# Output projections of a two-layer encoder trunk: two plain blocks and seven pairs, sums of the rows on GpSimd

## The chip, the cores and the metric

One core of one Trainium2 chip runs the whole program. The metric is the device time of one execution in microseconds: the median of the runs, 2163.85 for the kernel before (three runs, 2161.11 to 2164.45). The profile is of one further execution, with a time of its own.

## The reference

Two batches (256 and 512 rows, 768 together) go through an even and an odd layer of width 2048 with the same weights, in float32. Each layer ends with one output projection, whose result is added to the layer's input:

```
z = _rmsnorm(x, g) @ w_in
... the branches: attention and Fourier mixing (even), short convolution and spatial gate (odd),
... each multiplied by its SiLU gate
return x + jnp.concatenate([a, fo], axis=-1) @ w_out       # even
return x + jnp.concatenate([co, so], axis=-1) @ w_out      # odd
```

The concatenated, gated rows are what the change is about: 2048 features by 768 rows, which a 2048 x 2048 matrix multiplies.

## The kernel before

Everything stands transposed: a row block k of 128 features is a tile of 128 partitions by 768 rows, in two halves of 384 (s = 0, 1). There are 16 row blocks and 16 output blocks b. For precision each operand is split into a high and a low part: `split` (L130 to L132) copies on ScalarE (L131, hi) and subtracts on VectorE (L132, lo), and `three` (L117) issues three matmuls for every product. Weights come by DMA into `wr`, are split into `wh` and `wl` of 512 columns, and `Weights.ahead` does so four tiles before TensorE uses one (`RING`).

Blocks are made in two ways. *Plain*: `Stream.duo` takes two output blocks at once, 16 row blocks by 2 halves by 2 outputs by 3 matmuls, 192 in all, with 8 weight tiles. *In pairs*: `strassen` makes a pair of output blocks from seven products of half the size (Winograd's form): 7 x 8 x 3 = 168 matmuls with 14 weight tiles, of which four products first sum weights on VectorE (L196 to L202). Its left operands are the quarters of the rows, A11, A12, A21, A22 (feature half by row half), and three sums, S1 = A21 + A22, S2 = S1 - A11, S3 = A11 - A21; the seventh product needs S4 = A12 - S2, which here stands in the place of A21. The order of the products is A11, S1, S2, A12, S3, A22, S4. The sums must be formed and split before the first pair.

`Out.run` makes an output projection: two duos (blocks 0 to 3), then six pairs. Before the duos `load_cat` fills the slots of all 32 half row blocks from the stored gated rows (`cat`) and splits them; row blocks still on chip (`kept`) are split from there. Beside the first duo `build_sums` loads the rows a second time, into the slots of the sums; VectorE forms the four sums (L394 to L397) and splits three; the fourth, S4, is stored to memory (`s4d`, L398). Before the second duo everything pending is issued (`pipe.flush`). During the second duo, `done` loads S4 back into the place of A21 and splits it. In the even projection the slots of the sums (numbers 64 to 111) lie in the pool `late`, which takes over the memory of the attention's pool, tile by tile as those come free. In the odd projection `move` gives each quarter and sum the slots of operands of the pair before, in the order in which that pair frees them (`FREED`).

What sets the order: TensorE's is that of the program. The other engines and the DMA queue (all DMAs go out on SP) are put in order by a planner that goes by the order of the program and by what is ready in its own estimate. Generators spawned on `pipe` are stepped when the TensorE time counted in the program has come, so a helper's place in the program is between certain matmuls. In the even projection the result also gets squared on ScalarE (L786, L789) and added up on GpSimd (L790), for the norm of the odd layer.

Of the kernel before, what the change touches and what calls it, by code (L numbers as in the profile page):

```python
# [10 lines left out]
F32 = mybir.dt.float32  # L11
# [15 lines left out]
HT = H // P  # L27
BUILD = (4, 5, 6, 7, 0, 1, 2, 3)
BUILD_AT = 5.0
WIDTH = (TP, TS)  # L30
RING = 4
LOOK = 4
PLAIN = (0, 1, 2, 3)
PAIRS_E = ((8, 9), (10, 11), (12, 13), (14, 15), (4, 5), (6, 7))
PAIRS_O = ((4, 5), (6, 7), (8, 9), (10, 11), (12, 13), (14, 15))
PW = T + 4
# [56 lines left out]
def trunk(ctx, tc, x_t, w_in_e, w_fn, w_out_e, w_in_o, w_sv, w_out_o, w_f, w_st, b_s, sink, rel_bias,  # L93
# [62 lines left out]
    class Weights:  # L156
# [65 lines left out]
    def out_order(src, layer, pairs):  # L222
        plain = [(src, layer, b, q) for i in range(0, len(PLAIN), 2) for q in range(4) for b in PLAIN[i:i + 2]]
        return plain + [(src, layer, b, q) for b in pairs for q in range(14)]
# [30 lines left out]
    def x_slots(k, s):  # L255
        xs[k][s] = slots(quarter(k, s))
# [104 lines left out]
    kept = {}  # L361

    def load_cat(order):
        for k, s in order:
            x_slots(k, s)
            if k in kept:
                split(*xs[k][s], kept[k][:, SL[s]])
            else:
                fill(k, s, cat[k][:, SL[s]])
        kept.clear()  # L370
# [3 lines left out]
    def ev():  # L374
        return late[0].tile([P, H], F32, name="ev", bufs=4)
# [30 lines left out]
    def fill(k, h, src, g=None):  # L406
        at = where[quarter(k, h)]
        t = slot(at[1], F32)
        nc.sync.dma_start(out=t, in_=src)
        at[1], spare[0] = spare[0], at[1]  # L410
        x_slots(k, h)
        if g is None:
            split(*xs[k][h], t)
        else:
            split_gain(k, h, t, g)

    class Out:

        def __init__(self, n, pairs, first, last, res, result):
            self.n, self.pairs, self.res, self.result = n, pairs, res, result
            self.tags = (first, last, first)

        def run(self):
            st = Stream(self.n)

            def load(k, h, t):
                nc.sync.dma_start(out=t, in_=cat[k][:, SL[h]])

            def done(k, s):
                if s == 1 and k < KH:
                    fill(k, 1, s4d[k])

            pipe.spawn(build_sums(load, sums, BUILD, BUILD_AT))
            for i, tags in zip(range(0, len(PLAIN), 2), self.tags):
                duo = PLAIN[i:i + 2]
                last = i + 2 == len(PLAIN)
                if last:
                    pipe.flush()  # L440
                st.duo(duo, tags, done if last else None)
                for b in duo:
                    for h, z in enumerate(st.take(b)):
                        res = ev()
                        nc.sync.dma_start(out=res, in_=self.res[b][:, SL[h]])
                        nc.vector.tensor_add(out=res, in0=z, in1=res)
                        self.result(b, h, res)
            lent[0] = True
            for b in self.pairs:
                self.r = [big(i)[:, :T] for i in range(2)]  # L450
                for r, c in zip(self.r, b):
                    nc.sync.dma_start(out=r, in_=self.res[c])
                strassen(self.n, b, sums, ev, self, self.tags[-1])
            lent[0] = False
# [18 lines left out]
    def strassen(n, b, sums, ev, sink, tags):  # L473


        left = (
            [xs[j][0] for j in range(KH)], sums[1], sums[2], [xs[j + KH][0] for j in range(KH)],
            sums[3], [xs[j + KH][1] for j in range(KH)], [xs[j][1] for j in range(KH)],
        )
        acc = {}  # L480
        for i, at in enumerate((0, 2, 1, 0, 1, 3, 2)):
# [3 lines left out]
            for half in range(2):  # L485
                w = weights.at[n, b, 2 * i + half]
                weights.ahead(w + RING)
                for k in range(4):
                    j = 4 * half + k
                    three(acc[at], cols(weights.tiles[w], k), left[i][j], first and j == 0, j == KH - 1, not first)  # L490
                    pipe.tick()
# [172 lines left out]
    with tc.tile_pool(name="attn", bufs=1) as pool:  # L664
# [115 lines left out]

        load_cat([(k, s) for k in range(KT) for s in range(2)])

# [12 lines left out]
    sums = {i: [None] * KH for i in (1, 2, 3)}  # L795
    Out(1, PAIRS_E, (4, 5, 6, 7), (0, 1, 2, 3), x_t, keep_sum).run()

# [35 lines left out]
    if True:  # L833
# [124 lines left out]
    sums = {i: [None] * KH for i in (1, 2, 3)}  # L958
    Out(3, PAIRS_O, (0, 1, 2, 3), (4, 5, 6, 7), x1, finish).run()

# [79 lines left out]
```

## Time and profile before

| | |
|---|---|
| median of 3 runs | 2163.85 us |
| profiled execution | 2162.2 us, its span 2160.4 us |
| TensorE busy | 2120.9 us, 98% of the span, 12034 matmuls |
| VectorE busy | 1429.5 us, 66% |
| ScalarE busy | 898.9 us, 42% |
| GpSimd busy | 75.0 us, 3%, 75 instructions |
| granted TensorE clock | 0.995 on the mean |

The span runs from the first to the last instruction in the profile; the execution's time is 1.8 us longer. TensorE's share is an average: what matters for this change are two stretches, the even output projection (from about 790 to 1053 us) and the odd one (from about 1890 to the end). In the rows, `PE` is TensorE, `DVE` VectorE, `ACT` ScalarE, `POOL` GpSimd, `SPq` the DMA queue.

### The profile page before, as it was taken

To read this page: it belongs to the slowest core of one execution; us is meant where nothing else is said; L and a number is where in the kernel's file an instruction comes from. 1 tells how busy PE (TensorE), PEld (TensorE's weight loads), DVE (VectorE), ACT (ScalarE), POOL (GpSimd) and SP (SyncE) were. 2 spreads that over 40 slices of the span, in tenths; PEclk is the share of its full clock that TensorE was granted. 3 is DMA by queue.
4 is the path that set the end of the run, shared out by engine and by line. 5 is a ranking of instruction groups with operands and counts; after the bars stand their busy time and mean duration, and the time that the engine had idled before them with its cause. 6 is when DMAs were issued, how large, how long until landed. Compare 5 with 4: busy or idle time off the path is not lost.

```text
span 2160.4 us, 31653 instructions
## 1 busy us (share of the span) xinstructions
PE 2120.9 (98%) x12034; PEld 2074.6 (96%) x12034; DVE 1429.5 (66%) x2466; ACT 898.9 (42%) x1761; POOL 75.0 (3%) x75
## 2 busy tenths in 40 slices
PE   7999999999999998999899999999999999999999
PEld 5899999999999998999888999999999999999999
DVE  8535755745746768666795666666666777796665
ACT  6323443443444464333544433333334554553332
POOL 5000000000000000122100000000000000000000
PEclk9999999999999999999999999999999999999999
DMA  6522112122122148344946322222222332494342
GB/s 220 145 71 77 59 65 76 50 75 66 59 66 76 49 158 275 109 137 137 312 169 194 114 72 86 86 86 76 76 76 86 105 105 97 132 305 153 119 135 74
DMA packets 116512, 250.03 MB, mean 116 GB/s; under 512 B 12636, under 2 KB 72200, under 8 KB 116360
## 3 DMA queue, kind: packets, MB, share of 16 engines
q1 hardware_dynamic: 116360, 248.01, 35.3%
q8 instruction: 94, 1.54, 0.3%
q14 instruction: 58, 0.48, 0.1%
HBM read 210.19 MB, written 40.91 MB: 116 GB/s over the span
## 4 chain that ended last, share of the span: by engine, by line
PE 90%; DVE 3%; DMA 3%; ACT 2%; issue 1%; SPq 0%; DVEq 0%; ACTq 0%
PE bank L117 89%; DMA slot<-cat 1%; PE bank L127 1%; DMA xr<-in_x_t_dram 1%; DMA s<-slot 1%; DVE slot L268 1%; DVE slot L132 1%; DVE wl L132 0%; ACT sc L730 0%; DVE slot L395 0%; DVE slot L397 0%; ACT L730 0%; ACT L350 0%; DVE slot L396 0%; DVE slot L394 0%
## 5 line engine op out<-in xcount | busy, mean ns | idle before, releaser
L117 PE MATMUL bank<-slot,wh 128*128 128x384 f32 x6848 | 1747.0, 336 | 1.3 <-DVE ev L504 1.2
L117 PEld LDWEIGHTS bank<-slot,wh 128*128 128x128 f32 x6848 | 1236.1, 188 | 2.1 <-issue 1.5
L117 PE MATMUL bank<-slot,wl 128*128 128x384 f32 x3424 | 1150.0, 336 | 8.3 <-DVE wl L132 8.3
L131 ACT CAST wh<-wr 128x512 fp32r<-128x512 f32 x728 | 447.9, 620 | 875.8 <-PE bank L117 698.7
L132 DVE TENSOR_TENSOR wl<-wr,wh 128x512 fp32r<-128x512 f32 x728 | 504.8, 697 | 364.2 <-ACT wh L131 351.5
L117 PEld LDWEIGHTS bank<-slot,wl 128*128 128x128 f32 x3424 | 643.4, 188 | 9.6 <-DVE wl L132 9.6
L117 PE MATMUL bank<-wh,slot 128*128 128x512 f32 x576 | 187.1, 403 | 11.3 <-DVE slot L268 5.9
L117 PEld LDWEIGHTS bank<-wh,slot 128*128 128x128 f32 x576 | 111.0, 193 | 37.8 <-DVE slot L268 7.6
L131 ACT CAST slot<-slot 128x384 fp32r<-128x384 f32 x176 | 87.2, 512 | 108.0 <-DVE slot L132 37.4
L132 DVE TENSOR_TENSOR slot<-slot,slot 128x384 fp32r<-128x384 f32 x176 | 97.3, 557 | 31.9 <-ACT slot L131 24.3
L117 PE MATMUL bank<-wl,slot 128*128 128x512 f32 x288 | 115.3, 401 | 1.1 <-DVE wl L132 1.1
L689 DVE RECIPROCAL nrt<-nrt 128x384 f32<-128x384 f32 x32 | 81.6, 2549 | 4.8 <-ACT nrt L688 4.8
L117 PEld LDWEIGHTS bank<-wl,slot 128*128 128x128 f32 x288 | 55.7, 193 | 13.7 <-DVE wl L132 1.6
L345 DVE TENSOR_TENSOR row<-bank,rr 128x384 f32<-128x384 f32 x40 | 22.3, 557 | 39.6 <-PE bank L117 39.6
L200 DVE TENSOR_TENSOR wr<-wr 128x1024 f32<-128x1024 f32 x36 | 47.6, 1322 | 1.2
L202 DVE TENSOR_TENSOR wr<-wr 128x1024 f32<-128x1024 f32 x36 | 44.1, 1226 | 1.2
L196 DVE TENSOR_TENSOR wr<-wr 128x1024 f32<-128x1024 f32 x36 | 44.0, 1221 | 0.5
L198 DVE TENSOR_TENSOR wr<-wr 128x1024 f32<-128x1024 f32 x36 | 43.9, 1220 | 0.4
L790 POOL TENSOR_TENSOR rr<-rr,slot 128x384 f32<-128x384 f32 x24 | 35.3, 1473 | 130.2 <-ACT slot L789 130.2
L502 DVE TENSOR_TENSOR ev<-bank,ev 128x384 f32<-128x384 f32 x36 | 20.1, 558 | 28.7 <-PE bank L117 28.7
L507 DVE TENSOR_TENSOR ev<-ev,bank 128x384 f32<-128x384 f32 x36 | 19.9, 554 | 28.6 <-PE bank L117 28.6
L268 DVE SCALAR_TENSOR_TENSOR slot<-xr,sm,slot 128x384 fp32r<-128x384 f32 x32 | 36.5, 1184 | 3.2 <-ACT slot L267 3.2
(170 smaller groups left out, 1391.6 us busy)
## 6 DMA issues: line engine op xcount, KB each, us to landing
wr<-in_w_in_o_dram SPq DMA_DIRECT2D x96, 512.0 KB, 3.7
wr<-in_w_in_e_dram SPq DMA_DIRECT2D x72, 512.0 KB, 3.7
slot<-cat SPq DMA_DIRECT2D x120, 192.0 KB, 4.2
wr<-in_w_out_e_dram SPq DMA_DIRECT2D x32, 512.0 KB, 3.9
wr<-in_w_out_o_dram SPq DMA_DIRECT2D x32, 512.0 KB, 3.9
slot<-x SPq DMA_DIRECT2D x64, 192.0 KB, 4.2
wr<-in_w_sv_dram SPq DMA_DIRECT2D x16, 512.0 KB, 4.6
xr<-in_x_t_dram SPq DMA_DIRECT2D x15, 384.0 KB, 5.5
```

Of the source, the lines that this page charges most:

```text
L117: nc.tensor.matmul(out, lhsT=lhs, rhs=rhs, start=start, stop=stop, skip_group_check=go_on)
L127: nc.tensor.transpose(out=out, in_=in_, identity=ident)
L131: nc.scalar.copy(out=hi, in_=src)
L132: nc.vector.tensor_sub(out=lo, in0=src, in1=hi.bitcast(F32))
L196: nc.vector.tensor_sub(out=w11, in0=w12, in1=w11)
L198: nc.vector.tensor_sub(out=w11, in0=w22, in1=w11)
L200: nc.vector.tensor_sub(out=w12, in0=w22, in1=w12)
L202: nc.vector.tensor_sub(out=w21, in0=w11, in1=w21)
L268: nc.vector.scalar_tensor_tensor(out=lo, in0=src, scalar=g, in1=hi.bitcast(F32), op0=ALU.mult, op1=ALU.subtract)
L345: nc.vector.tensor_mul(out=out[:, SL[s]], in0=z[s], in1=rr[:, SL[s]])
L689: nc.vector.reciprocal(out=rt, in_=rt)
L790: nc.gpsimd.tensor_add(out=rr[:, SL[h]], in0=rr[:, SL[h]], in1=sq)
```

## The change

Both projections make one duo (blocks 0 and 1) and seven pairs. The rows are loaded once: `load_cat` loads each half row block as it is (`raws`) into the first four of the six slots of its sums, and splits from there into the slots of the quarters; rows still on chip are split by `split_kept`. `form`, begun 10 us (even) or 4 us (odd) after the duo starts, makes S1 on VectorE and S2, S3 and S4 on GpSimd, and splits S1. `place`, begun after the duo's eighth row block, splits S2, S4 and S3 of one row block after the other. S4 is not stored any more. In the odd projection the slots freed first now go to the sums.

```diff
-PLAIN = (0, 1, 2, 3)
-PAIRS_E = ((8, 9), (10, 11), (12, 13), (14, 15), (4, 5), (6, 7))
-PAIRS_O = ((4, 5), (6, 7), (8, 9), (10, 11), (12, 13), (14, 15))
+BUILD_E, BUILD_O = (4, 5, 6, 7, 0, 1, 2, 3), range(8)
+PLAIN = (0, 1)
+PAIRS_E = ((8, 9), (10, 11), (12, 13), (14, 15), (2, 3), (4, 5), (6, 7))
+PAIRS_O = ((2, 3), (4, 5), (6, 7), (8, 9), (10, 11), (12, 13), (14, 15))
...
+    def split_kept():
+        for k in sorted(kept):
+            for s in range(2):
+                x_slots(k, s)
+                split(*xs[k][s], kept[k][:, SL[s]])
     def load_cat(order):
         for k, s in order:
-            x_slots(k, s)
-            if k in kept:
-                split(*xs[k][s], kept[k][:, SL[s]])
-            else:
-                fill(k, s, cat[k][:, SL[s]])
+            j = k % KH
+            i = ((0, 1) if k < KH else (3, 2))[s]
+            t = raws[j, i] = slot([o for r in ("S1", "S2", "S3") for o in where[r, j]][i], F32)
+            nc.sync.dma_start(out=t, in_=cat[k][:, SL[s]])
+            if k not in kept:
+                x_slots(k, s)
+                split(*xs[k][s], t)
...
+        def form(self):
+            self.t = {}
+            for j in self.build:
+                ids = self.ids[j]
+                a0, a1, b1, b0 = (raws[j, i] for i in range(4))
+                nc.vector.tensor_add(out=b1, in0=a1, in1=b1)
+                t = self.t[j] = slot(ids[4], F32)
+                nc.gpsimd.tensor_sub(out=t, in0=b1, in1=a0)
+                nc.gpsimd.tensor_sub(out=a1, in0=a0, in1=a1)
+                nc.gpsimd.tensor_sub(out=b0, in0=b0, in1=t)
+                self.put(1, j, b1, ids[5])
+                spare[0] = ids[2]
+                yield 1.0
+        def place(self):
+            for j in self.build:
+                ids = self.ids[j]
+                self.put(2, j, self.t[j], ids[0])
+                spare[0] = ids[4]
+                x_slots(j, 1)
+                split(*xs[j][1], raws[j, 3])
+                self.put(3, j, raws[j, 1], ids[3])
+                spare[0] = ids[1]
+                yield 2.6
         def run(self):
             st = Stream(self.n)
             def done(k, s):
-                if s == 1 and k < KH:
-                    fill(k, 1, s4d[k])
-            pipe.spawn(build_sums(load, sums, BUILD, BUILD_AT))
+                if s == 1 and k == KH - 1:
+                    pipe.spawn(self.place(), 0.5)
+            pipe.spawn(self.form(), self.begin)
+            st.duo(PLAIN, self.first, done)
...
-        load_cat([(k, s) for k in range(KT) for s in range(2)])
+        split_kept()
...
+    load_cat([(k, s) for k in range(KT) for s in range(2)])
+    Out(1, PAIRS_E, BUILD_E, 10.0, (4, 5, 6, 7), (0, 1, 2, 3), x_t, keep_sum).run()
...
-        move("A11", "A21", "A12", "A22", "S1", "S2", "S3")
+        move("S1", "S2", "S3", "A11", "A21", "A12", "A22")
+        split_kept()
...
+    Out(3, PAIRS_O, BUILD_O, 4.0, (0, 1, 2, 3), (4, 5, 6, 7), x1, finish).run()
```

## Rows read from the trace of the kernel before

**Rows 1.** The page, part 4: shares of the chain that ended last, by engine.
```profile
PE 90%; DVE 3%; DMA 3%; ACT 2%; issue 1%; SPq 0%; DVEq 0%; ACTq 0%
```

**Rows 2.** Timeline of GpSimd in the even pairs: start, us, engine, line, operation [idle before].
```profile
895.86 1.01 POOL L790 TENSOR_TENSOR rr<-rr,slot 128x384 f32<-128x384 f32 x1 [5.01 <-ACT slot L789]
...
925.01 1.02 POOL L790 TENSOR_TENSOR rr<-rr,slot 128x384 f32<-128x384 f32 x1 [13.88 <-ACT slot L789]
```

**Rows 3.** Timeline of TensorE, even projection and just after it.
```profile
847.77 0.44 PE L117 MATMUL bank<-slot,wl 128*128 128x384 f32 x1 [3.06 <-DVE wl L132]
851.18 0.69 PE L117 MATMUL bank<-slot,wl 128*128 128x384 f32 x1 [2.62 <-DVE wl L132]
...
1057.12 1.22 PE L117 MATMUL bank<-wh,slot 128*128 128x512 f32 x2 [3.79 <-DVE slot L268]
```

**Rows 4.** Timeline of VectorE ahead of the even projection.
```profile
786.16 0.56 DVE L345 TENSOR_TENSOR row<-bank,rr 128x384 f32<-128x384 f32 x1 [1.52 <-PE bank L117]
...
806.55 0.95 DVE L354 TENSOR_TENSOR at<-row,at 128x768 f32<-128x768 f32 x1
```

**Rows 5.** Windows: length, busy us of PE, PEld, DVE, ACT, POOL (instructions), PEclk, DMA, GB/s.
```profile
2100.00:2129.16 29.16, 29.16 (x170) 29.16 (x169) 18.73 (x28) 9.09 (x15) 0.00 (x0) 1.00 0.33 109
850.00:855.00 5.00, 3.82 (x12) 3.82 (x13) 4.65 (x9) 3.21 (x7) 1.99 (x1) 0.50 0.88 285
787.00:851.00 64.00, 58.51 (x336) 57.87 (x335) 54.83 (x107) 37.17 (x76) 3.04 (x2) 0.98 0.88 291
1894.00:1957.30 63.30, 59.50 (x340) 58.50 (x338) 59.84 (x123) 30.16 (x62) 0.00 (x0) 1.00 0.85 281
```

**Rows 6.** Timeline of TensorE, odd projection: its waits.
```profile
1907.31 0.59 PE L117 MATMUL bank<-slot,wh 128*128 128x384 f32 x2 [1.18 <-DVE ev L504]
...
1921.86 0.44 PE L117 MATMUL bank<-slot,wl 128*128 128x384 f32 x1 [0.93 <-DVE wl L132]
...
1957.27 0.44 PE L117 MATMUL bank<-slot,wl 128*128 128x384 f32 x1 [1.69 <-DVE wl L132]
```

**Rows 7.** The page, part 6: DMA issues, count, KB each, us to landing.
```profile
slot<-cat SPq DMA_DIRECT2D x120, 192.0 KB, 4.2
...
slot<-s SPq DMA_DIRECT2D x24, 192.0 KB, 3.6
```

**Rows 8.** Timeline of ScalarE: the last product of attention.
```profile
777.84 0.48 ACT L752 COPY at<-bank 128x384 f32<-128x384 f32 x1 [0.62 <-PE bank L117]
```

**Rows 9.** Timeline of VectorE in the odd projection's first duo.
```profile
1926.88 0.69 DVE L132 TENSOR_TENSOR wl<-wr,wh 128x512 fp32r<-128x512 f32 x1
1927.49 0.55 DVE L132 TENSOR_TENSOR slot<-slot,slot 128x384 fp32r<-128x384 f32 x1
1927.96 0.68 DVE L132 TENSOR_TENSOR wl<-wr,wh 128x512 fp32r<-128x512 f32 x1
```

**Rows 10.** Timelines of VectorE and GpSimd in an even pair.
```profile
904.15 1.22 DVE L196 TENSOR_TENSOR wr<-wr 128x1024 f32<-128x1024 f32 x1
905.40 1.92 DVE L200 TENSOR_TENSOR wr<-wr 128x1024 f32<-128x1024 f32 x1
...
904.19 2.05 POOL L790 TENSOR_TENSOR rr<-rr,slot 128x384 f32<-128x384 f32 x1 [1.21 <-ACT slot L789]
```

**Rows 11.** Timeline of all engines in the even projection's second duo.
```profile
849.28 2.70 POOL L790 TENSOR_TENSOR rr<-rr,ev 128x384 f32<-128x384 f32 x1 [4.28 <-ACT ev L789]
849.50 0.55 DVE L397 TENSOR_TENSOR slot<-slot,slot 128x384 f32<-128x384 f32 x1
...
851.24 1.16 DVE L132 TENSOR_TENSOR slot<-slot,slot 128x384 fp32r<-128x384 f32 x1
```

**Rows 12.** Timeline of all engines at the kernel's start.
```profile
15.33 8.75 POOL L536 TENSOR_TENSOR acc<-acc,sq 128x768 f32<-128x768 f32 x4 [0.41 <-ACT sq L534]
...
18.04 6.98 DVE L268 SCALAR_TENSOR_TENSOR slot<-xr,sm,slot 128x384 fp32r<-128x384 f32 x4
...
25.54 1.14 DVE L268 SCALAR_TENSOR_TENSOR slot<-xr,sm,slot 128x384 fp32r<-128x384 f32 x2
```

More of the change, by code (lines that the diff above doesn't have):

```diff
@@ L27 @@
 HT = H // P
-BUILD = (4, 5, 6, 7, 0, 1, 2, 3)
-BUILD_AT = 5.0
+BUILD_E, BUILD_O = (4, 5, 6, 7, 0, 1, 2, 3), range(8)
 WIDTH = (TP, TS)
@@ L222, in out_order @@
     def out_order(src, layer, pairs):
-        plain = [(src, layer, b, q) for i in range(0, len(PLAIN), 2) for q in range(4) for b in PLAIN[i:i + 2]]
+        plain = [(src, layer, b, q) for q in range(4) for b in PLAIN]
         return plain + [(src, layer, b, q) for b in pairs for q in range(14)]
@@ L361, in trunk @@
     kept = {}
+    raws = {}
+    def split_kept():
[3 more added lines that the diff above has]
+                split(*xs[k][s], kept[k][:, SL[s]])
     def load_cat(order):
         for k, s in order:
-            x_slots(k, s)
-            if k in kept:
-                split(*xs[k][s], kept[k][:, SL[s]])
-            else:
-                fill(k, s, cat[k][:, SL[s]])
+            j = k % KH
[5 more added lines that the diff above has]
+                split(*xs[k][s], t)
         kept.clear()
@@ L417, in trunk, with __init__ @@
     class Out:
-        def __init__(self, n, pairs, first, last, res, result):
-            self.n, self.pairs, self.res, self.result = n, pairs, res, result
-            self.tags = (first, last, first)
+        def __init__(self, n, pairs, build, begin, first, last, res, result):
+            self.n, self.pairs, self.build, self.res, self.result = n, pairs, build, res, result
+            self.begin, self.first, self.last = begin, first, last
+            self.ids = {j: [i for r in ("S1", "S2", "S3") for i in where[r, j]] for j in build}
@@ new lines, in put @@
+        def put(self, i, j, src, hi):
+            where[f"S{i}", j] = [hi, spare[0]]
+            sums[i][j] = slots((f"S{i}", j))
+            split(*sums[i][j], src)
+        def form(self):
[11 more added lines that the diff above has]
+                yield 1.0
@@ L425, in run @@
+        def place(self):
[8 more added lines that the diff above has]
+                yield 2.6
         def run(self):
             st = Stream(self.n)
-            def load(k, h, t):
-                nc.sync.dma_start(out=t, in_=cat[k][:, SL[h]])
@@ L431, in done @@
             def done(k, s):
-                if s == 1 and k < KH:
-                    fill(k, 1, s4d[k])
-            pipe.spawn(build_sums(load, sums, BUILD, BUILD_AT))
[L436 to L447, printed above, removed]
+                if s == 1 and k == KH - 1:
+                    pipe.spawn(self.place(), 0.5)
@@ L448, in run @@
+            pipe.spawn(self.form(), self.begin)
+            st.duo(PLAIN, self.first, done)
+            for b in PLAIN:
+                for h, z in enumerate(st.take(b)):
+                    res = ev()
+                    nc.sync.dma_start(out=res, in_=self.res[b][:, SL[h]])
+                    nc.vector.tensor_add(out=res, in0=z, in1=res)
+                    self.result(b, h, res)
             lent[0] = True
@@ L452, in run @@
                     nc.sync.dma_start(out=r, in_=self.res[c])
-                strassen(self.n, b, sums, ev, self, self.tags[-1])
+                strassen(self.n, b, sums, ev, self, self.last)
             lent[0] = False
@@ L473, in strassen, with left @@
     def strassen(n, b, sums, ev, sink, tags):
[L476 to L479, printed above, removed]
+        def left(i, j):
+            if i in (1, 2, 4):
+                return sums[i if i < 4 else 3][j]
+            return xs[j + KH * (i in (3, 5))][i >= 5]
         acc = {}
@@ L489, in strassen @@
                     j = 4 * half + k
-                    three(acc[at], cols(weights.tiles[w], k), left[i][j], first and j == 0, j == KH - 1, not first)
+                    three(acc[at], cols(weights.tiles[w], k), left(i, j), first and j == 0, j == KH - 1, not first)
                     pipe.tick()
@@ L795, in trunk @@
     sums = {i: [None] * KH for i in (1, 2, 3)}
-    Out(1, PAIRS_E, (4, 5, 6, 7), (0, 1, 2, 3), x_t, keep_sum).run()
+    load_cat([(k, s) for k in range(KT) for s in range(2)])
+    Out(1, PAIRS_E, BUILD_E, 10.0, (4, 5, 6, 7), (0, 1, 2, 3), x_t, keep_sum).run()
     xhat = [dram.tile([P, T], F32, name=f"xhat{k}") for k in range(KT)]
@@ L958, in trunk @@
     sums = {i: [None] * KH for i in (1, 2, 3)}
-    Out(3, PAIRS_O, (0, 1, 2, 3), (4, 5, 6, 7), x1, finish).run()
+    Out(3, PAIRS_O, BUILD_O, 4.0, (0, 1, 2, 3), (4, 5, 6, 7), x1, finish).run()
 def _t5_onehot():
```

## The prediction

> **What bounds the kernel now.** I read the page first: TensorE holds 90% of the chain that ended last [rows 1]. So a gain has to be fewer matmuls, or one of TensorE's few waits gone. Then the timelines, for the price of a matmul. In the paired stage the sums for the norm on GpSimd come at 895.86 and, one pair later, at 925.01 [rows 2]: 29.15 us for a pair of 7 x 2 x 4 x 3 = 168 matmuls, 0.1735 us each. VectorE works 18.73 us of such a period [rows 5], so in the steady pairs it follows easily.
>
> The two output projections begin with something else, and there TensorE does wait. In the even one it stands 3.06 and then 2.62 us for VectorE's weight split (wl) [rows 3]. How much this costs in all: the block before the projection ends at 786.1 (its result is taken then, after a wait for TensorE) [rows 4]. One more block of 96 matmuls, 16.7 us, puts the start of the first duo at 802.8. The six pairs end at 1057.12 - 3.79 = 1053.3 [rows 3], and last six periods plus the 0.7 us by which their last one is longer, 175.6: they began at 877.7. Two duos of 192 matmuls would take 66.6; they took 74.9. So 8.3 us are lost, 5.7 of it in the two waits, the rest (2.6) at the lower clock: 850 to 855 is granted 0.50, the 1.2 GHz level, just after TensorE had stood [rows 5]. In the odd projection there are three waits, 1.18, 0.93 and 1.69 us, 3.8 together, and no drop of the clock shows [rows 6]. Lost in both: 12.1 us.
>
> All of these waits end with VectorE, so I read that engine in both stretches. From 787 to 851 it is busy 54.8 of 64 us, with the DMA engines at 0.88; from 1894 to 1957.3 it is busy 59.8 of 63.3 [rows 5]. The even stretch is VectorE plus loads that come late, the odd one VectorE alone.
>
> **The change, part by part.** *Matmuls.* A duo goes and a pair comes in each projection: 192 - 168 = 24 matmuls, 24 x 0.1735 = 4.2 us, twice: **8.3 us** off TensorE. The added pair brings 14 weight splits, 4 weight sums and its evictions where the duo had 8 splits and 4 evictions; a pair leaves VectorE 10 us free [rows 5], so they are hidden.
>
> *DMA.* Of 120 loads of gated rows 64 remain, and 16 of the 24 round trips of the fourth sum through memory go [rows 7]. This takes away what kept VectorE waiting in the even stretch, but only as far as its own work lets it: I treat it below as working without such gaps. The rows of the even projection now go into the late pool, which takes over the attention's memory. Attention's last product is copied out at 777.84 [rows 8], nine us before the first slots for split rows come free, so I count these loads as early. The rows of the last gate (at 806.55 [rows 4]) can't be; what stands behind them on SP's queue comes up to 9 us later if the queue keeps the written order. I take nothing for it and keep it for the upper end.
>
> *VectorE and GpSimd.* This decides. Now only one duo (33.3 us) lies ahead of the first pair, whose third product needs S2, formed on GpSimd. VectorE's operations on 384 columns follow each other every 0.47 us, weight splits every 0.61 [rows 9]. Even projection, from 787 to the moment when the last S2 is read (its last built row is the fourth: 802.8 + 33.3 + 8.3 + 1.6 = 846.0), 59.0 us: 32 splits of the rows (15.0), 16 weight splits (9.8), 2 weight sums of 1.22 [rows 10] (2.4), 2 gates of 0.95 and 2 row scalings [rows 4] (2.8), 8 additions and 8 splits of S1 (7.5), 22 of the 24 splits of S2, S4, S3 (10.3), 4 evictions (1.9): 49.7 us. Odd projection: the last product of the pair before begins at 1907.31 [rows 6], so the duo starts at 1911.5 and the last S2 is due at 1911.5 + 33.3 + 8.3 + 3.6 = 1956.7. The slots of the split rows come free from the fourth product on, about 1894: 62.7 us for 32 row splits (15.0), 21 weight splits (12.8), 2 sums (2.4), the gating of the pair before (5.6), S1 (7.5), the 22 splits (10.3) and evictions (1.9): 55.5 us. Without GpSimd both fit, with 9.3 and 7.2 us to spare.
>
> But GpSimd isn't beside VectorE. In 22 operations before the last S2 it reads the same memory. Alone such an operation takes 1.01 us [rows 2]. What it takes from VectorE: at 904.19 GpSimd waits behind a VectorE sum (2.05 us instead of 1.01), then the next VectorE sum takes 1.92 instead of 1.22: **0.70 us** lost [rows 10]. At 849.28 it waits behind three short VectorE operations in a row (the first of them stands in the group) and then delays the next one by about 0.6 (1.16 against 0.55) [rows 11]. At the kernel's start, with GpSimd at work back to back, four VectorE operations took 6.98 us, where two more of the same kind a little later, with GpSimd idle, take 1.14 [rows 12]: 4.7 us lost. GpSimd worked beside them until 24.08, 6.04 us or 2.8 of its operations of 768 columns at 2.19: 1.7 us lost to each, and some 0.9 for 384 columns. So the loss per operation lies between 0 (GpSimd falls into VectorE's gaps) and 1.01 (blocked throughout). I take 0.70, from the one row with the same shape on GpSimd and a full VectorE.
>
> The Trainium skill (SBUF — State Buffer, section "Who interferes with whom") says that a VectorE instruction with both inputs in SBUF contends with a GpSimd instruction that reads there, and that the one that comes first holds the port for its whole length. Here the rows at 904 and 849 show just such a hand-over, and the price by that rule is the upper end, not 0.70; it speaks against this change, and the first rival is the time that it gives.
>
> 22 x 0.70 = 15.4. Even: 49.7 + 15.4 - 59.0 = 6.1 us late; odd: 55.5 + 15.4 - 62.7 = 8.2. Of VectorE's operations in both, 17 read a PSUM bank and one SBUF operand (8 us); GpSimd holds a quarter of the time, so some 2 us of them fall beside it. Late in all: 12.3 us. In the queues this shows as weight splits behind a split that waits for GpSimd, on ScalarE first, then VectorE; four weight tiles lie ready, 12 matmuls or 2.1 us each in a pair, which covers 8 us of waiting and no more. On GpSimd's queue behind the sums stand two additions of squares, whose buffers the first pair needs at its third product, 848.6; 24 operations from 811 end at 835 to 847 at 1.0 to 1.5 us each, so nothing is added.
>
> *Sum.* The waits of before go, 12.1, and as much comes back in the first pair, 12.3; what stays are the matmuls: -8.3 - 12.1 + 12.3 = **-8.1 us**. From the profiled execution's 2162.2 (span 2160.4 and 1.8 around it) this is 2154.1; the median of the runs stands 1.65 above it, so 2155.8, rounded to **2156**.
>
> **The rivals.** *The shared port takes more than it gives (slower).* One VectorE operation for each GpSimd operation, as at the start. At 1.01 per operation: even 12.9 late, odd 15.0, less 3 us of PSUM reads beside, plus the lower clock once more (2.6): 27.5. -8.3 - 12.1 + 27.5 = +7.1: **2171**. It decides in the duo, where the weight splits of the first pair stand behind nine splits that wait for GpSimd. The break-even is at a loss of 0.89 us per operation (44 of them make 39, of which 16.5 fit the spare time and 2.5 the PSUM reads; the 20.4 left are all that is gained). For it: [rows 12], with 0.9. Against it: [rows 11], where three VectorE operations passed while GpSimd waited.
>
> *No new wait.* GpSimd runs in gaps, or the S2 splits come ahead of S3 and S4, which aren't due until 8 and 17 us later. Then both the matmuls and the waits are gained: -20.4, **2143.5**. For it: 17 us of spare time in both stretches together. Against it: 31 us of GpSimd operations at 0.70 don't fit into that.
>
> *The rows come late.* If the even projection's loads wait for the last gate at 806.55 and not for attention's last read, VectorE's work begins 20 us later than 787; some 5 us of it (gates, weights) needs no rows, so 15 us more wait and the lower clock: **2174**. Against it: the late pool waits tile by tile. This would also mean that the change does not do what it says, load early.
>
> **How the numbers follow.** Chances: the forecast 0.48, with a range of its own of 2150 to 2162 (a loss of 0.55 to 0.85 per operation); no new wait 0.20; the port 0.25, from 2162 to 2172; late rows 0.07. The range that takes in both ends of the unknown price is 2144 to 2172. A measurement of this kernel can tell 0.2%, 4.3 us, from no change: faster is below 2159.5, slower above 2168.2. Faster: three quarters of the forecast's 0.48 and all of 0.20, 0.56. Same: a fifth of 0.48 and four tenths of 0.25, 0.20. Slower: the rest, 0.24.
>
> **What would show it.** Right: TensorE with 48 matmuls fewer in all; 64 loads of rows, 8 round trips left; 48 more GpSimd operations, most of them 1.0 to 2.1 us; VectorE's 384-column splits in the duos longer than 0.55 on the mean; no TensorE wait inside the duos, and some 5 to 8 us of waits in each first pair, at the second or third product, with VectorE named. Wrong: TensorE without a gap there (no new wait); gaps of over 10 us with a clock of 0.50 behind them, and a VectorE that does one operation per GpSimd operation (the port); a gap ahead of the even duo that ends with a load (late rows).

## The result, and the profile after

The kernel after takes 2193.52 us (median of four runs, 2191.10 to 2193.96) against 2163.62 for the kernel before beside it: 1.0138 times as long, 95% interval 1.012 to 1.0155. It is 30 us slower; the prediction was 8 us faster. The profiled execution took 2193.46 us, its span 2191.4.

Busy time and counts from the page of after (part 1), then the chain (part 4), then the groups (part 5: busy us and mean ns of one, then the idle time before them):

```profile
PE 2124.9 (97%) x11986; PEld 2075.6 (95%) x11986; DVE 1458.8 (67%) x2448; ACT 907.6 (41%) x1775; POOL 140.4 (6%) x123
...
PE 88%; DMA 3%; DVE 3%; ACT 2%; issue 2%; POOL 1%; SPq 0%; POOLq 0%; DVEq 0%; ACTq 0%
...
L131 DVE TENSOR_TENSOR slot<-slot,slot 128x384 fp32r<-128x384 f32 x176 | 112.8, 669 | 29.4 <-ACT slot L130 21.7
...
slot<-cat SPq DMA_DIRECT2D x64, 192.0 KB, 4.3
```

The counts are those of the change: 48 matmuls fewer, 48 GpSimd instructions more, 64 loads of rows where [rows 7] had 120. But VectorE, with 18 instructions fewer, is busy 29 us longer: its 384-column splits take 0.669 us on the mean where they took 0.557.

TensorE's timeline, around both first duos and first pairs; it answers to [rows 3] and [rows 6]. In brackets: idle before the instruction, and what ended it.

```profile
810.58 1.28 PE L116 MATMUL bank<-slot,wh 128*128 128x384 f32 x2 [7.69 <-ACT slot L130]
...
848.17 0.69 PE L116 MATMUL bank<-slot,wl 128*128 128x384 f32 x1 [9.14 <-DVE wl L131]
850.85 0.69 PE L116 MATMUL bank<-slot,wl 128*128 128x384 f32 x1 [1.35 <-DVE wl L131]
...
866.38 0.61 PE L116 MATMUL bank<-slot,wh 128*128 128x384 f32 x2 [2.19 <-ACT wh L130]
869.19 0.69 PE L116 MATMUL bank<-slot,wl 128*128 128x384 f32 x1 [2.19 <-DVE wl L131]
...
1958.51 0.61 PE L116 MATMUL bank<-slot,wh 128*128 128x384 f32 x2 [3.71 <-ACT wh L130]
1962.71 0.69 PE L116 MATMUL bank<-slot,wl 128*128 128x384 f32 x1 [3.59 <-DVE wl L131]
1966.38 0.69 PE L116 MATMUL bank<-slot,wl 128*128 128x384 f32 x1 [2.34 <-DVE wl L131]
...
1985.11 0.69 PE L116 MATMUL bank<-slot,wl 128*128 128x384 f32 x1 [4.06 <-DVE wl L131]
```

There are two kinds of gap. One of 7.69 us stands *ahead of* the even duo and ends with a row's cast (L130), the first half of its split. All others end with a weight's cast or subtraction. They make 22.6 us in the even projection and 13.7 in the odd, in rows shown. The gaps at 848.17 and 850.85, and those from 1958.51 to 1966.38, lie inside the duos: 10.5 and 9.6 us where the prediction had none.

What late rows look like: SP's queue ahead of the even duo.

```profile
805.38 0.33 SPq L340 DMA_DIRECT2D cat<-at  x1
805.80 17.25 SPq L376 DMA_DIRECT2D slot<-cat  x32
```

All 32 loads go out in one row, right behind the last gate's store.

VectorE's timeline: the first split of a loaded row, then splits and additions beside GpSimd's subtractions (x8: eight instructions in 10.32 us), a weight split, and, in the odd projection, the first additions of S1 (L448) and a split that waits for GpSimd's S2 (L450).

```profile
810.56 6.38 DVE L131 TENSOR_TENSOR slot<-slot,slot 128x384 fp32r<-128x384 f32 x12 [3.60 <-ACT slot L130]
...
832.13 10.32 DVE L131 TENSOR_TENSOR slot<-slot,slot 128x384 fp32r<-128x384 f32 x8
842.38 3.08 DVE L448 TENSOR_TENSOR slot<-slot,slot 128x384 f32<-128x384 f32 x3
845.38 1.34 DVE L131 TENSOR_TENSOR slot<-slot,slot 128x384 fp32r<-128x384 f32 x1
846.64 1.48 DVE L131 TENSOR_TENSOR wl<-wr,wh 128x512 fp32r<-128x512 f32 x1
...
1937.83 1.49 DVE L448 TENSOR_TENSOR slot<-slot,slot 128x384 f32<-128x384 f32 x3
...
1952.21 1.33 DVE L131 TENSOR_TENSOR slot<-slot,slot 128x384 fp32r<-128x384 f32 x1 [1.94 <-POOL slot L450]
```

GpSimd's timeline: the first and the last of its 24 subtractions in each projection, and two in the middle of the even one.

```profile
824.58 1.09 POOL L450 TENSOR_TENSOR slot<-slot,slot 128x384 f32<-128x384 f32 x1 [768.59 <-DVE slot L448]
...
831.75 1.33 POOL L450 TENSOR_TENSOR slot<-slot,slot 128x384 f32<-128x384 f32 x1
833.05 1.33 POOL L451 TENSOR_TENSOR slot<-slot,slot 128x384 f32<-128x384 f32 x1
...
854.17 1.33 POOL L452 TENSOR_TENSOR slot<-slot,slot 128x384 f32<-128x384 f32 x1
...
1938.62 2.67 POOL L450 TENSOR_TENSOR slot<-slot,slot 128x384 f32<-128x384 f32 x1 [335.17 <-ACT wh L130]
...
1968.12 1.31 POOL L452 TENSOR_TENSOR slot<-slot,slot 128x384 f32<-128x384 f32 x1
```

From 832.13 to 842.38 VectorE starts eight operations, 1.28 us apart; alone they stand 0.47 apart [rows 9]. GpSimd starts one every 1.28 us in the same time (eight from 831.75 to 842.00). The windows show the same as turns, one to one: five to five in 5 us, both engines wholly busy (columns as in [rows 5]).

```profile
830.00:835.00 5.00, 5.00 (x31) 5.00 (x30) 4.97 (x5) 3.61 (x8) 5.00 (x5) 1.00 0.02 7
...
845.00:850.00 5.00, 1.33 (x3) 0.82 (x3) 5.00 (x5) 1.53 (x3) 5.00 (x5) 0.50 0.17 44
...
1938.00:1970.00 32.00, 22.36 (x112) 21.21 (x112) 26.39 (x24) 12.49 (x27) 30.82 (x24) 0.84 0.15 49
1960.00:1970.00 10.00, 4.95 (x14) 4.44 (x15) 8.19 (x7) 2.94 (x7) 9.43 (x8) 0.50 0.34 104
```

Where both queues are full, each GpSimd subtraction thus costs VectorE 1.28 - 0.47 = 0.81 us. This is about the gap of 9.14 us: the weight split at 846.64 stands behind twelve operations from 832.13 on, which take 14.5 us; at 0.47 each they would take 5.6, 8.9 less (an estimate). After TensorE has stood, the granted clock is 0.50, the 1.2 GHz level, at 845 to 850 and again at 1960 to 1970. In the odd projection ScalarE hands the delay on: in its order a row's cast waits for GpSimd, and the weight casts stand behind it, the first of them released TensorE's wait of 3.71 us at 1958.51.

```profile
1957.01 0.93 ACT L130 CAST slot<-slot 128x384 fp32r<-128x384 f32 x2 [1.63 <-POOL slot L451]
1957.84 1.13 ACT L130 CAST wh<-wr 128x512 fp32r<-128x512 f32 x2
```

For the comparisons below the profiled execution is cut at three points that every kernel has: VectorE's last row scaling of the block ahead of the last gate (786.16 in [rows 4]), ScalarE's first square root behind the even projection (1069.30 in the kernel before), VectorE's last eviction (2156.87). The even stretch is the first to the second, the odd one the second to the third.

| kernel | S2 to S4 | even rows | duos even, odd | median us | even | odd |
|---|---|---|---|---|---|---|
| before | VectorE | twice | 2, 2 | 2163.6 | 283.1 | 1087.6 |
| after | GpSimd | once | 1, 1 | 2193.5 | 303.2 | 1098.7 |
| e1 | VectorE | once | 1, 1 | 2168.9 | 293.6 | 1085.4 |
| e2 | GpSimd | twice | 1, 1 | 2192.5 | 301.5 | 1098.5 |
| e3 | VectorE | twice | 1, 1 | 2163.7 | 287.0 | 1083.9 |
| e4 | GpSimd | once | 2, 2 | 2186.5 | 297.7 | 1096.1 |
| e5 | GpSimd, constants | once | 1, 1 | 2151.9 | 283.4 | 1078.4 |
| e8 | GpSimd, copies | once | 1, 1 | 2167.2 | 289.8 | 1086.2 |
| e9 | GpSimd, constants | twice | 1, 1 | 2152.7 | 283.5 | 1078.5 |
| e10 | GpSimd, constants | once, GpSimd's queue | 1, 1 | 2146.9 | 276.2 | 1078.4 |
| e11 | VectorE | once, GpSimd's queue | 1, 1 | 2161.9 | 287.4 | 1083.9 |
| e6 | VectorE | twice | 2, 2 | 2161.7 | 284.1 | 1088.1 |
| e7 | VectorE | twice | 2, 1 | 2159.7 | 283.4 | 1085.4 |
| e12 | VectorE | once, GpSimd's queue | 2, 1 | 2159.0 | 283.7 | 1084.0 |

e2 and e4 are single timings; the medians of the kernel before beside the runs lay between 2162.1 and 2165.1. The stretches are those of one execution each, so they can differ by some us from what the medians say. e5, e8, e9 and e10 leave S2, S3 and S4 out: they are probes, not versions that could be used.

### The profile page after: what moved, and what is told of

Same layout as the page of the kernel before. It is cut to its first block, busy times and chain, and to the rows that moved or that the text cites. A ratio compares the mean times of both kernels' runs of the same rounds, so it can differ in the third digit from the quotient of the medians.

```text
span 2191.4 us, 31481 instructions
## 1 busy us (share of the span) xinstructions
PE 2124.9 (97%) x11986; PEld 2075.6 (95%) x11986; DVE 1458.8 (67%) x2448; ACT 907.6 (41%) x1775; POOL 140.4 (6%) x123
## 4 chain that ended last, share of the span: by engine, by line
PE 88%; DMA 3%; DVE 3%; ACT 2%; issue 2%; POOL 1%; SPq 0%; POOLq 0%; DVEq 0%; ACTq 0%
PE bank L116 87%; DVE slot L131 2%; DMA bias_d<-vec_d 1%; PE bank L126 1%; DMA xr<-in_x_t_dram 1%; DMA slot<-cat 0%; ACT slot L266 0%; DVE slot L267 0%; DMA slot<-x 0%; POOL slot L450 0%; DVE wl L131 0%; POOL slot L452 0%; ACT sc L766 0%; DMA row<-in_seq_s_dram 0%; DMA x<-ev 0%
## 5 line engine op out<-in xcount | busy, mean ns | idle before, releaser
L116 PEld LDWEIGHTS bank<-slot,wh 128*128 128x128 f32 x6816 | 1236.9, 189 | 15.3 <-ACT slot L130 8.0
L130 ACT CAST wh<-wr 128x512 fp32r<-128x512 f32 x740 | 455.9, 620 | 924.5 <-PE bank L116 728.5
L131 DVE TENSOR_TENSOR wl<-wr,wh 128x512 fp32r<-128x512 f32 x740 | 518.0, 703 | 366.3 <-ACT wh L130 361.6
L116 PE MATMUL bank<-wh,slot 128*128 128x512 f32 x576 | 188.0, 404 | 12.3 <-DVE slot L267 6.7
L131 DVE TENSOR_TENSOR slot<-slot,slot 128x384 fp32r<-128x384 f32 x176 | 112.8, 669 | 29.4 <-ACT slot L130 21.7
L130 ACT CAST slot<-slot 128x384 fp32r<-128x384 f32 x176 | 84.7, 511 | 88.6 <-POOL slot L451 24.7
L450 POOL TENSOR_TENSOR slot<-slot,slot 128x384 f32<-128x384 f32 x16 | 22.2, 1384 | 1104.3 <-DVE slot L448 769.1
L826 POOL TENSOR_TENSOR rr<-rr,slot 128x384 f32<-128x384 f32 x28 | 41.6, 1486 | 160.0 <-ACT slot L825 160.0
L199 DVE TENSOR_TENSOR wr<-wr 128x1024 f32<-128x1024 f32 x38 | 50.7, 1334 | 1.2
L201 DVE TENSOR_TENSOR wr<-wr 128x1024 f32<-128x1024 f32 x38 | 46.5, 1225 | 1.3
L195 DVE TENSOR_TENSOR wr<-wr 128x1024 f32<-128x1024 f32 x38 | 46.3, 1219 | 0.5
L197 DVE TENSOR_TENSOR wr<-wr 128x1024 f32<-128x1024 f32 x38 | 46.4, 1220 | 0.4
```

The lines of the kernel that those rows point to most:

```text
L116: nc.tensor.matmul(out, lhsT=lhs, rhs=rhs, start=start, stop=stop, skip_group_check=go_on)
L195: nc.vector.tensor_sub(out=w11, in0=w12, in1=w11)
L197: nc.vector.tensor_sub(out=w11, in0=w22, in1=w11)
L199: nc.vector.tensor_sub(out=w12, in0=w22, in1=w12)
L201: nc.vector.tensor_sub(out=w21, in0=w11, in1=w21)
L450: nc.gpsimd.tensor_sub(out=t, in0=b1, in1=a0)
```

## The experiments

**Who forms the sums, and where the rows come from (e1 to e4).** e1 puts the three subtractions on VectorE:

```diff
-                nc.gpsimd.tensor_sub(out=t, in0=b1, in1=a0)
+                nc.vector.tensor_sub(out=t, in0=b1, in1=a0)
...
```

> The changed kernel, but S2, S3 and S4 are formed on VectorE as S1 is; nothing else differs. Theory (the shared read port): GpSimd's 24 operations per projection cost VectorE about 0.8 us each and ScalarE's queue waits for them; on VectorE they cost 0.47 each. Then VectorE's splits go back from 0.67 to 0.55 us on the mean, the odd projection loses some 4 us instead of 18.9, the even one some 17 instead of 31 (its late rows stay): about 2165 us. Rival (one duo is too short a time, or the late rows are the whole loss): the work is only moved, the waits stay: 2185 or more.

Measured: 2168.86 us, 1.0028 of before (1.0016 to 1.0040), 24.7 us less than after: near the 2165 expected and far from the rival's 2185. VectorE's splits are back at 0.553 us; the wait ahead of the even duo stays. TensorE's waits of e1, even:

```profile
810.00 1.28 PE L116 MATMUL bank<-slot,wh 128*128 128x384 f32 x2 [7.62 <-ACT slot L130]
839.84 0.44 PE L116 MATMUL bank<-slot,wl 128*128 128x384 f32 x1 [1.68 <-DVE wl L131]
...
858.34 1.01 PE L116 MATMUL bank<-slot,wh 128*128 128x384 f32 x2 [3.94 <-ACT wh L130]
```

GpSimd's help is worth less than nothing. e2 keeps it and loads the even rows early into their own slots, and a second time for the sums, as the kernel before:

```diff
-        split_kept()
+        load_early([(k, s) for k in range(KT) for s in range(2)])
...
-    load_cat([(k, s) for k in range(KT) for s in range(2)])
+    load_cat([(k, s) for k in range(KT) for s in range(2)], True)
```

> The changed kernel, but in the even projection the rows are loaded twice as in the kernel before: first into free slots of the rows and split from there, then again into the slots of the sums. GpSimd's sums stay. Theory (late rows): TensorE's wait of 7.7 us ahead of the even duo goes, and VectorE gets 15 us of splits done ahead of the duo; the even projection loses some 11 us instead of 31: about 2173. Rival (the port decides in the even projection too): only the first wait goes, 10 us with the clock, and it is partly given back behind GpSimd: 2184 to 2190.

Measured: 2192.45 us in one timing. The expected 2173 fell. The wait ahead of the duo is gone, and its time comes back in the first pair, whose first two products wait for weights (TensorE, e2):

```profile
846.82 1.01 PE L116 MATMUL bank<-slot,wh 128*128 128x384 f32 x2 [6.28 <-ACT wh L130]
851.39 0.69 PE L116 MATMUL bank<-slot,wl 128*128 128x384 f32 x1 [3.57 <-DVE wl L131]
```

e3 does both.

> Both: sums on VectorE, and the even projection's rows loaded twice. If the port and the late rows are the two causes and one duo is long enough for VectorE, both projections lose about 4 us: some 2153, under the kernel before. Rival (one duo is too short for the work whichever engine does it): waits of over 8 us in each first pair: 2165 or more.

Measured: 2163.66 us, 1.0008 of before (0.9998 to 1.0018), not the 2153 expected. Undoing both takes back the 30 us. The 8.3 us of matmuls still don't show: in the odd stretch 3.7 us are gained, but the even one is 3.9 longer. Waits of 8.67 and 3.44 us for weight splits and casts stand in the first pair, so one even duo is too short for VectorE's work even so; e11 below shows the like without the second loads. TensorE, e3:

```profile
844.13 0.69 PE L116 MATMUL bank<-slot,wl 128*128 128x384 f32 x1 [8.67 <-DVE wl L131]
853.12 0.61 PE L116 MATMUL bank<-slot,wh 128*128 128x384 f32 x2 [3.44 <-ACT wh L130]
```

e4 keeps the sums on GpSimd and gives back the second duo (six pairs), `PLAIN = (0, 1, 2, 3)`, with the loops that go with it.

> The changed kernel, but with two duos and six pairs as before (8.3 us more matmuls); GpSimd forms the sums in the first duo, and their splits are placed in the second. Theory (the sums on GpSimd only come too late for one duo): with 33 us more the odd projection loses some 4 us instead of 18.9, and the even one some 12 (the late rows) instead of 31: about 2168. Rival (GpSimd's operations slow VectorE wherever they lie, and the weights with it): the waits move into the second duo and stay, 14 us or more in the odd projection: 2190 or more.

Measured: 2186.49 us in one timing: 7 us less than after, not 25, though with 8.3 us more of matmuls. A wait of 8.72 us at 847.69 and one of 7.17 at 1957.16 stand at the same places as in after, in the first duo. More time ahead of the pairs takes some 15 us of the waits away and doesn't cure them.

**What of GpSimd's work costs (e5, e8).** e5 lets GpSimd write and not read, so that S2, S3 and S4 are not formed:

```diff
-                nc.gpsimd.tensor_sub(out=t, in0=b1, in1=a0)
+                nc.gpsimd.memset(t, 0.5)
...
```

> GpSimd writes a constant into the three buffers instead of subtracting, so S2 to S4 are not computed; every wait on GpSimd stays, only its reads go. Theory (GpSimd's two-input reads halve VectorE's rate): the 384-column splits go back from a mean of 0.67 us to 0.55 to 0.58, VectorE does not fall to one operation per 1.29 us, and the time is 2160 to 2167, no more than with the sums on VectorE (2168.9), because VectorE also has the 48 subtractions less. Rival one (what costs is the chain VectorE, GpSimd, ScalarE, VectorE with its queues, whatever GpSimd reads): 2185 to 2193. Rival two (any GpSimd instruction on this memory, also one that only writes, takes VectorE's turn): splits at 0.63 to 0.67 and 2178 to 2193.

Measured: 2151.91 us, 0.9944 of before (0.9930 to 0.9957), 41.6 us less than after and 17 less than e1. VectorE's eight splits from 823.08 follow each other every 0.47 us, though two of GpSimd's constants fall beside them (824.63 and one at 826.04), and no TensorE wait but the one for the rows is left in the even duo. VectorE, GpSimd and TensorE of e5:

```profile
823.08 3.83 DVE L131 TENSOR_TENSOR slot<-slot,slot 128x384 fp32r<-128x384 f32 x8
826.83 0.55 DVE L448 TENSOR_TENSOR slot<-slot,slot 128x384 f32<-128x384 f32 x1
...
824.63 0.42 POOL L452 MEMSET slot<- 128x384 f32 x1 [0.94 <-DVE slot L131]
...
809.15 1.28 PE L116 MATMUL bank<-slot,wh 128*128 128x384 f32 x2 [7.82 <-ACT slot L130]
```

The expectation overlooked that writing t needs no addition first, so GpSimd's chain also ends early. e8 puts that chain back, with one input read instead of two:

```diff
-                nc.gpsimd.tensor_sub(out=t, in0=b1, in1=a0)
-                nc.gpsimd.tensor_sub(out=a1, in0=a0, in1=a1)
-                nc.gpsimd.tensor_sub(out=b0, in0=b0, in1=t)
+                nc.gpsimd.tensor_copy(out=t, in_=b1)
+                nc.gpsimd.tensor_copy(out=a1, in_=a0)
+                nc.gpsimd.tensor_copy(out=b0, in_=t)
```

> GpSimd copies instead of subtracting: t from b1, a1 from a0, b0 from t, so S2 to S4 are not computed. Unlike the run that only wrote constants, each copy reads memory, and the first still waits for VectorE's addition and the third for the first, as the subtractions did. Theory (what costs is that a GpSimd read in the shared memory takes VectorE's turn, operation for operation): with one input read instead of two the operation is shorter but still alternates with VectorE; 384-column splits at a mean of 0.60 to 0.67 us, time 2170 to 2193. Rival one (only a two-input GpSimd operation does so): splits at 0.55 to 0.57, time 2150 to 2160, as with the constants. Rival two (the constants were harmless because they came out of the chain of waits early, and the chain is what costs): VectorE's splits back at 0.55, yet the time 2175 to 2193, with TensorE's waits of 2 to 9 us in the even duo back.

Measured: 2167.22 us, 1.0016 of before (1.0006 to 1.0025), splits at 0.594. A little under the expected 2170, but neither rival. VectorE and GpSimd of e8; the copy at 825.44 had VectorE idle beside it, the one at 831.78 not:

```profile
828.28 6.28 DVE L131 TENSOR_TENSOR slot<-slot,slot 128x384 fp32r<-128x384 f32 x8
834.49 1.79 DVE L448 TENSOR_TENSOR slot<-slot,slot 128x384 f32<-128x384 f32 x3
...
825.44 0.50 POOL L450 COPY slot<-slot 128x384 f32<-128x384 f32 x1
...
831.78 0.83 POOL L450 COPY slot<-slot 128x384 f32<-128x384 f32 x1
```

The turns are there too, 0.78 us apart (828.28 to 834.49, eight of them), so a copy costs VectorE 0.31 where both queues are full. The three kernels make a scale, since VectorE has the same 2448 instructions in each: their pages have it busy 1425.1 us with constants, 13.1 more with copies and 33.7 more with subtractions, on the mean 0.27 and 0.70 us for each of the 48 operations. Not every one of them meets a VectorE operation. The windows of both stretches (columns as in [rows 5]), first of after, then of e5:

```profile
786.29:1089.46 303.17, 273.90 (x1497) 268.64 (x1496) 215.17 (x302) 137.61 (x253) 77.77 (x54) 0.94 0.48 159
1089.46:2188.14 1098.68, 1084.53 (x6056) 1058.37 (x6054) 774.53 (x1256) 430.83 (x820) 32.13 (x48) 0.99 0.34 110
...
784.73:1068.14 283.41, 268.09 (x1497) 263.73 (x1496) 196.87 (x303) 135.37 (x253) 56.67 (x54) 0.97 0.52 170
1068.14:2146.58 1078.44, 1078.26 (x6056) 1054.05 (x6054) 759.24 (x1254) 430.15 (x820) 11.37 (x48) 1.00 0.34 112
```

With subtractions VectorE is busy 18.3 us longer in the even stretch and 15.3 in the odd, and these take 19.8 and 20.2 us more; with copies it is 7.4 and 5.4 us, and 6.4 and 7.8 more. In the odd one VectorE also stands for GpSimd's S2 (the wait at 1952.21 and four like it, 5.6 us together), so there the time is not the lost turns alone. e1 gives the price of VectorE's time without GpSimd: its subtractions keep VectorE busy 11.3 us longer than in e5 in either stretch, and these take 10.2 and 7.0 us more. For TensorE, of the 40.0 us between e5 and after, 27.9 are time in which it stands, and 12.1 are the same matmuls at a lower clock (granted 0.94 and 0.99 on the mean, against 0.97 and 1.00).

**The late rows by themselves (e9 to e11).** e9 is e5 with e2's early loads.

> GpSimd only writes constants (S2 to S4 are not computed), and the even rows are loaded early and a second time, as in the kernel before. With the run that only wrote constants (2151.9) it prices the late rows by themselves. Theory (the late rows cost the wait of 7.8 us ahead of the even duo and the clock after it, some 11 us, since VectorE has no other work to catch up): 2139 to 2144, the wait at 809 gone and no wait over 2 us in the even duo. Rival (what the late rows take is spare time, and the second loads bring the waits of the kernel before back in the duo): 2148 to 2154.

Measured: 2152.68 us, 0.9943 (0.9927 to 0.9960), no gain over e5: the theory's 2139 to 2144 fell. The wait at 809 is gone, and waits of 0.5 to 2.6 us in the first pair stand for it; the time is the rival's. From 810 to 820 the DMA engines are at 0.98 and VectorE is busy 4.57 of 10 us: the 64 loads now seem to set the pace. So this didn't price the order in SP's queue. e10 does, by sending the 32 loads through GpSimd's own queue:

```diff
-            nc.sync.dma_start(out=t, in_=cat[k][:, SL[s]])
+            (nc.gpsimd if lent[1] else nc.sync).dma_start(out=t, in_=cat[k][:, SL[s]])
...
-    load_cat([(k, s) for k in range(KT) for s in range(2)])
+    lent.append(True)
+    load_cat([(k, s) for last in (0, 1) for k in range(KT) for s in range(2) if (k in kept) == last])
+    lent[1] = False
```

> As the run that only wrote constants (S2 to S4 are not computed; 2151.9), but the even projection's 32 loads go out on GpSimd's DMA queue instead of SP's, the rows of the last gate last: loaded once, and not behind the last gate's store in SP's queue. Theory (the order in SP's queue alone kept the rows late; once and early costs nothing): first row splits on VectorE before 795 instead of 810, the wait of 7.8 us at 809 gone, 2140 to 2146. Rival one (the rows are kept back by the memory that they take over or by the DMA engines, whatever the queue): wait of 6 us or more still there, 2149 to 2155. Rival two (issuing 32 loads from GpSimd takes time from it or from VectorE): 2150 to 2165.

> The same loads on GpSimd's queue, with all three sums computed, on VectorE: one duo, rows once. Theory (the once-loaded rows, early, and no GpSimd reading beside VectorE): as the run with the sums on VectorE (2168.9) less 8 to 12 for the wait ahead of the even duo; VectorE's 24 subtractions of 0.47 then fill what comes free, so 2157 to 2162, TensorE waits of 2 to 6 us at the even duo's end. Rival (queue does not help): 2166 to 2170.

Measured: e10 2146.89 us, 0.9929 (0.9916 to 0.9943), just above the expected 2140 to 2146 and 5.0 less than e5; e11 2161.93, 1.0005 (0.9995 to 1.0014), within its expectation and 6.9 less than e1. The even stretch is 7.2 us shorter than in e5, and 6.2 than in e1. GpSimd's queue, VectorE, TensorE, and a window of e10:

```profile
761.37 2.29 POOL L376 DMA_DIRECT2D slot<-cat  x4 [705.16 <-DVE ptl L782]
...
786.34 3.82 POOL L376 DMA_DIRECT2D slot<-cat  x7 [0.74 <-issue]
...
806.14 8.05 DVE L131 TENSOR_TENSOR slot<-slot,slot 128x384 fp32r<-128x384 f32 x17
...
806.04 0.44 PE L116 MATMUL bank<-slot,wh 128*128 128x384 f32 x1 [3.89 <-ACT slot L130]
...
823.00:829.00 6.00, 6.00 (x37) 6.00 (x36) 6.00 (x14) 6.00 (x15) 6.00 (x18) 1.00 0.07 15
```

The first loads go out 44 us earlier, some of them even before 777.84 [rows 8], so memory was free as the prediction had it. But VectorE splits the first loaded row only at 806.14, not before 795 as expected: its own order, too, has the loaded rows behind the last gate. Of the wait, 3.9 us stay. The window is the clearest test of the constants: for 6 us VectorE and GpSimd are both wholly busy, GpSimd starts a constant every 0.36 us, and VectorE's 384-column operations still follow each other every 0.47 us.

**A version that beats both (e6, e7, e12).** All have the sums on VectorE. e6 has two duos in both projections.

> All three sums on VectorE, even rows loaded twice as before, and two duos with six pairs in both projections: the kernel before with the fourth sum kept on chip. Theory (one duo is too short for VectorE's work even without GpSimd, and the second duo gives back the 8 to 12 us that the even projection still waited): 8.3 us more matmuls than with one duo (2163.7), some 13 us of waits less in the even projection and 3 less in the odd: 2155 to 2160, TensorE waits of 3 to 6 us in the even duos at most. Rival (the loads at 285 to 291 GB/s set the even stretch, as in the kernel before, and the 16 round trips that are gone don't matter): 2162 to 2166, with the even waits of 3 and 2.6 us back.

Measured: 2161.69 us, 0.9993 (0.9984 to 1.0002), next to the rival's 2162: an even wait is back (5.76 us at 840.58), and the round trips that are gone bring nothing to see. e7 has two duos in the even projection and one in the odd, `DUOS = {1: (0, 1, 2, 3), 3: (0, 1)}`.

> As the run before in the even projection (two duos, sums on VectorE, rows loaded twice), but one duo and seven pairs in the odd one, rows loaded once, sums on VectorE. Theory (the odd stretch keeps the 2 to 3.7 us that it gained with the sums on VectorE, the even one costs what it cost in the kernel before or less): 2152 to 2160, faster than the kernel before by 0.15 to 0.5 per cent. Rival (the odd projection's gain was the second duo's absence alone and the even one's waits are the loads'): 2159 to 2163, no difference that can be told.

Measured: 2159.66 us, 0.9983 (0.9974 to 0.9991), faster than before by 3.3 us. The time lies in both expected ranges; that the difference can be told, the rival had not. e12 adds e10's queue for the even rows.

> Two duos in the even projection, one in the odd, sums on VectorE, as in the run that came to 2159.7, but the even rows are loaded once, on GpSimd's queue. Theory (with a second duo VectorE's sums have time, and 32 loads less take the wait of 5.3 us at 840 away; the wait of 3.9 us at 806 comes instead): 2156 to 2160, no wait over 2 us in the even duos. Rival (splits behind the last gate in VectorE's order push the same lateness into the second duo): 2160 to 2164, a wait of 4 us or more at 840 to 880 besides that at 806.

Measured: 2158.99 us, 0.9987 (0.9978 to 0.9996), within e7's interval. The wait at 840 is gone (0.85 us is left), and 3.88 at 805.94 stands in its place. Both are faster than the kernel before by 0.1 to 0.2%; which is better can't be told.

## Why the prediction was wrong

*Matmuls, DMA counts: right.* 48 fewer, 64 loads, 8 round trips, as the page of after and its list of DMA issues have them.

*"I take nothing for it" (rows behind the last gate): wrong.* The paragraph had named the danger, that what stands behind the last gate's rows on SP's queue comes up to 9 us later, and priced it at nothing. All 32 loads stood there, at 805.80, and VectorE's first split of one came at 810.56 where the sum has it working from 787. The rival for late rows was right in the place, the last gate, and too large (15 us and the clock); what it weighed against itself, that memory comes free tile by tile, was true and didn't help, since the order in the queue decided. By that order, e10 against e5 and e11 against e1 show 7.2 and 6.2 us in the even stretch (5.0 and 6.9 in the medians, on different chips); by the wait left in e10, the engines' own order some 4 more.

*The loss per operation, 0.70: right on the mean, in part by luck.* VectorE's busy time gives 33.7 us for 48 operations, 0.70 each, where the sum had 30.8 for 44. Yet it is 0.81 where both queues are full and less where VectorE has gaps, and [rows 10] showed neither: one GpSimd operation against a much longer VectorE sum. With short operations on both sides they take turns, as at the kernel's start [rows 12], and the three that passed a waiting GpSimd [rows 11] were no guide to a full queue. By the prediction's own break-even, 0.89, the change would still have gained, so the fault lies in what was taken off the loss.

The Trainium skill (SBUF — State Buffer, "Who interferes with whom") says that such a VectorE instruction contends with a GpSimd one that reads, and not with one that only writes; e5, e8 and e10 agree, with 0 us lost beside constants and 0.31 beside copies. It also says (section "SBUF: two separate sides") that of two such operations the first gets the shared pair for its whole instruction; the rows give less, 0.81 us of 1.01 for a subtraction and 0.31 of 0.50 for a copy.

*"Both fit, with 9.3 and 7.2 us to spare": the step that failed.* From the 30.8 us that GpSimd was to take, the sum took off 16.5 of spare time and 2 for reads from PSUM, a term that no run prices, and kept 12.3 of waits at the full clock. Measured, VectorE lost 33.7 us, and the two stretches are 40.0 us longer than with constants (41.6 by the medians). e1 says the same without GpSimd: 22.5 us more work on VectorE make them 17.2 us longer. So little or nothing of the spare time shows in the time. Two terms were put at nothing besides: 5.6 us in which VectorE stands for GpSimd's S2 in the odd projection, and 12.1 us of matmuls at the lower clock. Whether spare time was there and the slow matmuls made up for it, or whether the slow matmuls only stand in place of further waits, the runs don't separate.

The sum also set the wrong deadline. It let every operation move into every hole of a stretch, up to the last read of S2. Here three orders forbid it. VectorE's additions stand behind its row splits, so GpSimd begins 14.0 us after the start of the even duo (824.58 against 810.58), where the prediction had 8, and some 9 us after that of the odd one (1938.62 against about 1930, where the last eviction of the pair before stands). On VectorE weight splits stand behind splits that take turns with GpSimd, so TensorE waits already inside the duo, at 848.17. And on ScalarE weight casts stand behind row casts that wait for GpSimd (1957.01). GpSimd's own end isn't what TensorE waits for in the odd projection: it comes at 1969.4, some 40 us after the duo's start, and the sum had the last S2 due after 45.

*The waits of before go, 12.1: nearly right.* With nothing lost to GpSimd and the rows early (e10) the time is 15.2 us under the kernel before; the rival "no new wait" had 20.4, and the wait of 3.9 us and the clock behind it (0.66 at 805 to 810) are most of the rest.

So, from the rival's -20.4: about +9 is what e5 still lacks, for the most part the late rows by e10; about +41 is what GpSimd's subtractions add to e5, lost turns, waits for its sums and the slower clock; together +30. The forecast's sign turned on two costs, one taken as nothing, the other reduced by time that did not show and reckoned at the full clock. The rival of the shared port named the place (weight splits behind splits that wait), the turns and the slower clock, with 2.6 us for it; it, too, subtracted the spare time, and so stopped at 2171. No rival reached the measured time; the highest, for late rows, had 2174.

## What to carry to other kernels

Moving an operation from VectorE to GpSimd pays only if GpSimd takes less of VectorE's time than the operation did: here 0.70 us on the mean, and 0.81 in full queues, were lost for 0.47 saved, though GpSimd had stood idle. Don't count spare time in a stretch without asking whether the engines' written orders let work into it, and price the slower clock behind each wait; look for what stands first in each queue, and price a load by the store and the waits ahead of it in its queue, not by when its memory comes free. When a phase is shortened, ask whether the helper engine's work for the next phase still fits in it: with the sums on VectorE, one duo less gained 3.7 us in the odd projection (e3), nearly its 4.2 of matmuls, and nothing in the even one.

## What had not been expected of the hardware

Beside a full VectorE queue a GpSimd operation that reads took much of its own length from VectorE, but not all: 0.81 us for a subtraction of 384 columns that takes 1.01 alone, 0.31 for a copy that takes 0.50, nothing for a constant of 0.42. Beside subtractions the two full queues took turns one to one, five to five in 5 us, so that VectorE's 384-column operations ran at 0.47 / 1.28 = 37% of their rate.
